# Second feed-forward block: seven half-size block products in place of eight, gated factors through DRAM

## Chip, cores and metric

The kernel runs on one core of a Trainium2 chip. The metric is device time in microseconds (us) from the first to the last instruction of one execution, including what the launch puts around it; of several runs the median is given. A profile of one execution shows TensorE (PE, and PEld for its weight loads), VectorE (DVE), ScalarE (ACT), GpSimd (POOL), and SyncE (SP), which issues nearly all DMAs here.

## What is computed

One encoder block on 1024 tokens of 1024 channels, f32: a feed-forward half, two token mixers (sparse attention and retention), their merge and out projection, a second feed-forward half, a gated embedding, and a final norm. What the change touches, cut from the reference:

```
def swiglu(x, w_gate, w_up, w_down):
    return (jax.nn.silu(x @ w_gate) * (x @ w_up)) @ w_down

h = h + merged @ w_out[i]
h = h + 0.5 * swiglu(rms_norm(h, ffn2_norm[i]), ffn2_w_gate[i], ffn2_w_up[i], ffn2_w_down[i])
gate = jax.nn.sigmoid(rms_norm(h, ple_norm[i]) @ w_ple_gate[i])
h = h + gate * (p[i] @ w_ple_proj[i])
return rms_norm(h, final_norm)
```

`w_gate` and `w_up` are 1024 x 2816, `w_down` 2816 x 1024.

## The kernel before

Every f32 product is made of three matmuls in the format float32r: each operand is split into a high part `h` (a rounded copy, by ACT) and a low part `l` (the rest, by DVE's subtraction), and `split3` (L246) names the three products high x high, high x low, low x high. A matmul takes a stationary 128x128 operand and a moving one of 128x512 and adds into one PSUM bank.

Weights come through the class `Weights` (L86): a list of jobs in the order of use, two raw buffers `wraw` of 128x1024 f32 into which SP loads (L104), and six pairs `wh`, `wl` into which ACT (L117) and DVE (L119, POOL for some jobs) split. When the last product that needs a pair has been issued, `release` gives it back and `pump` loads and splits what is next. PE's instructions stand in the order of the code; the order on the other engines and on SP's queue is set by a scheduler that orders instructions when the program is built.

The activations lie transposed (channels on partitions) in `uh` and `ul`: eight channel blocks by 1024 tokens. `turned` (L322) makes them: four transposes by PE into a bank of the tag `tr` (L328), then the split by ACT and DVE (L250, L251). `Norm.scaled` (L309) is the norm of one block of 128 tokens: ACT squares, a DVE operation, POOL's power, a DVE scaling (L315).

After the merge stage the out projection runs (L1154): for two halves of the channels and eight token blocks, 24 matmuls each (`product`, L288), added into the residual `hres` in SBUF (L1158), which was loaded from `hspill` in DRAM (L1150). In the second half each finished block is normed, and turned two blocks later.

The second FFN is `ffn` (L333), the same code as the first. For each of 22 blocks of 128 hidden units (`gate_up`, L338) and each half of the tokens it makes 24 matmuls for gate (`pg`), 24 for up (`pu`), then Silu on ACT (L354), the product on DVE (L355) and the split into `hh`, `hl`, which stay in SBUF. After every second block `down` (L360) multiplies two blocks into all 8 x 2 pieces of the output, six matmuls each (`pd`), and DVE adds every piece times 0.5 into the residual (L370). The last `down` norms each finished token block and weaves in transposes and the first products of the embedding gate (L1180 to L1185). Then come the embedding gate's products (`ple_gate`, L1170), `embedded`, and `finish` with the final norm and the store.

PSUM's eight banks are dealt out by `bank_plan`: three `mm`, three `dn`, two `tr` in this part.

## Time and profile before

| | |
|---|---|
| three runs | 2720.04, 2723.23, 2723.80 us; median 2723.23 |
| the profiled execution | 2723.87 us, its span 2722.1 us |
| granted TensorE clock, mean | 0.99 of full |
| PE busy | 2645.2 us, 12160 matmuls |
| PEld, DVE, ACT, POOL busy | 2149.6, 1375.9, 872.7, 335.2 us |
| DMA | 190.38 MB, mean 70 GB/s |

The page gives busy time as the union of an engine's instructions. Matmuls overlap in the pipeline and their ends are modelled, so a matmul's duration is longer than the distance to the next one. The chain of the page follows the work that ended last back from the end, from each instruction to what released it. In the views by stretch of time, windows are in us from the start of the span.

### The profile page before, as it was taken

What the parts mean: (1) busy time and instruction counts of PE and PEld (TensorE: products, weight loads), DVE (VectorE), ACT (ScalarE), POOL (GpSimd) and SP (SyncE); (2) the same over time, 40 slices, a digit from 0 to 9 for tenths busy, and PEclk for the clock granted to TensorE, in tenths of its full rate; (3) what the DMA queues carried; (4) which work ended last, traced back from release to release, by engine and by line L of the source; (5) the groups of instructions that cost most, each with busy time, mean ns of one, the idle gap of its engine ahead of it and who ended that gap; (6) DMA issues with size and microseconds to landing.
All of it is one profiled execution on the core that took longest, in us unless ns stands there. A gap on an engine that the chain in (4) does not pass through costs nothing.

```text
span 2722.1 us, 31668 instructions
## 1 busy us (share of the span) xinstructions
PE 2645.2 (97%) x12160; PEld 2149.6 (79%) x12160; DVE 1375.9 (51%) x2622; ACT 872.7 (32%) x1590; POOL 335.2 (12%) x308
## 2 busy tenths in 40 slices
PE   8999999999999998989999999999999999999998
PEld 6888888888888777767878877788888888888877
DVE  5433333333357879997457766524333333333364
ACT  5211111111135667652245654313111111111142
POOL 1000000000000333443344430000000000000000
PEclk9999999999999999999999999999999999999999
DMA  6111111111120221221221228531111111111122
GB/s 237 47 47 47 47 47 47 47 47 47 48 104 20 74 86 32 67 78 55 74 80 39 82 86 236 169 124 55 47 47 47 47 47 47 47 47 47 47 70 93
DMA packets 222487, 190.38 MB, mean 70 GB/s; under 512 B 12416, under 2 KB 186752, under 8 KB 222336
## 3 DMA queue, kind: packets, MB, share of 16 engines
q1 hardware_dynamic: 222336, 188.37, 22.9%
q8 instruction: 95, 1.56, 0.2%
q14 instruction: 56, 0.46, 0.1%
HBM read 154.78 MB, written 33.55 MB: 69 GB/s over the span
## 4 chain that ended last, share of the span: by engine, by line
PE 53%; DVE 8%; issue 3%; ACT 3%; POOL 2%; DMA 1%; SPq 0%; POOLq 0%; ACTq 0%; DVEq 0%
PE prod L288 11%; PE pu L244 9%; PE pg L244 9%; PE pd L244 9%; PE pgate L689 6%; PE pmrg L244 3%; DVE bias L755 1%; PE psc L244 1%; PE plg L244 1%; ACT bias L756 1%; PE ppt L1008 1%; PE ppv L1019 1%; DVE eq L758 1%; DMA sgl<-gspill 1%; DMA yparts<-yaspill 1%
## 5 line engine op out<-in xcount | busy, mean ns | idle before, releaser
L117 ACT ACTIVATE wh<-wraw 128x1024 fp32r<-128x1024 f32 (+1 forms) x224 | 234.4, 1056 | 857.5 <-PE pd L244 405.5
L370 DVE SCALAR_TENSOR_TENSOR hres<-pd,hres 128x512 f32<-128x512 f32 x352 | 240.7, 690 | 200.1 <-PE pd L244 199.5
L119 DVE TENSOR_TENSOR wl<-wraw,wh 128x1024 fp32r<-128x1024 f32 (+1 forms) x176 | 213.8, 1226 | 210.1 <-ACT wh L117 205.6
L355 DVE TENSOR_TENSOR sg<-sg,pu 128x512 f32<-128x512 f32 x88 | 60.5, 687 | 506.6 <-PE pu L244 506.6
L244 PE MATMUL pd<-wh,hh 128*128 128x512 f32 x704 | 279.1, 396 | 0.0
L244 PE MATMUL pg<-uh,wh 128*128 128x512 f32 x704 | 278.6, 396 | 0.2 <-ACT uh L250 0.2
L244 PE MATMUL pg<-ul,wh 128*128 128x512 f32 x704 | 278.5, 396 | 0.2 <-DVE ul L251 0.2
L244 PE MATMUL pu<-uh,wh 128*128 128x512 f32 x704 | 278.5, 396 | 0.0
L244 PE MATMUL pg<-uh,wl 128*128 128x512 f32 x704 | 278.5, 396 | 0.0
L244 PE MATMUL pu<-uh,wl 128*128 128x512 f32 x704 | 278.4, 396 | 0.0
L244 PE MATMUL pu<-ul,wh 128*128 128x512 f32 x704 | 278.4, 395 | 0.0
L244 PE MATMUL pd<-wl,hh 128*128 128x512 f32 x704 | 278.0, 395 | 0.0
L244 PE MATMUL pd<-wh,hl 128*128 128x512 f32 x704 | 278.0, 395 | 0.0
L288 PE MATMUL prod<-wh,uh 128*128 128x512 f32 (+1 forms) x648 | 265.2, 409 | 0.2 <-ACT gt L696 0.2
L288 PE MATMUL prod<-wh,ul 128*128 128x512 f32 (+1 forms) x648 | 257.1, 397 | 0.0
L288 PE MATMUL prod<-wl,uh 128*128 128x512 f32 (+1 forms) x648 | 256.7, 396 | 0.0
L314 POOL TENSOR_TENSOR nst<-nst,mhalf 128x1 f32<-128x1 f32 x32 | 17.9, 559 | 1590.0 <-DVE nst L313 1590.0
L689 PE MATMUL pgate<-uh,wh 128*128 128x512 f32 x384 | 158.7, 413 | 22.2 <-ACT gt L696 21.2
L244 PEld LDWEIGHTS pg<-ul,wh 128*128 128x128 f32 x704 | 132.2, 188 | 32.4 <-DVE ul L251 0.5
L244 PEld LDWEIGHTS pg<-uh,wh 128*128 128x128 f32 x704 | 132.3, 188 | 32.3 <-ACT uh L250 0.5
L244 PEld LDWEIGHTS pu<-uh,wl 128*128 128x128 f32 x704 | 132.2, 188 | 32.0
L244 PEld LDWEIGHTS pu<-ul,wh 128*128 128x128 f32 x704 | 132.2, 188 | 32.0
(225 smaller groups left out, 4684.4 us busy)
## 6 DMA issues: line engine op xcount, KB each, us to landing
wraw<-in_ffn_w_gate_dram SPq DMA_DIRECT2D x44, 512.0 KB, 3.9
wraw<-in_ffn_w_up_dram SPq DMA_DIRECT2D x44, 512.0 KB, 4.7
wraw<-in_ffn_w_down_dram SPq DMA_DIRECT2D x44, 512.0 KB, 3.4
wraw<-in_w_in_dram SPq DMA_DIRECT2D x32, 512.0 KB, 3.8
gspill<-gt SPq DMA_DIRECT2D x48, 256.0 KB, 2.1
wraw<-in_w_branch_b_dram SPq DMA_DIRECT2D x16, 512.0 KB, 4.4
sgl<-gspill SPq DMA_DIRECT2D x32, 256.0 KB, 3.4
wraw<-in_w_in_dram SPq DMA_DIRECT2D x18, 256.0 KB, 3.0
```

The source lines that it names most:

```text
L117: self.nc.scalar.activation(h[:, :n], t[:, :n], AF.Copy)
L119: eng.tensor_tensor(l[:, :n], t[:, :n], h[:, :n].bitcast(F32), op=OP.subtract)
L244: nc.tensor.matmul(ps, a, b, start=i == 0, stop=i == n - 1)
L288: nc.tensor.matmul(box[0][:, :cols], a, w, start=k == 0 and i == 0, stop=k == nk - 1 and i == 2)
L355: nc.vector.tensor_tensor(a, a, pu, op=OP.mult)
L370: nc.vector.scalar_tensor_tensor(hres[:, b, half(i)], pd, 0.5, hres[:, b, half(i)], op0=OP.mult, op1=OP.add)
L689: nc.tensor.matmul(box[0], a, m, start=k == 0 and j == 0, stop=k == KT - 1 and j == 2)
L755: nc.vector.tensor_scalar(m, x_, t[:, j:j + 1], None, op0=op)
L756: nc.scalar.activation(m, m, AF.Copy, accum_out=cnt[:, j:j + 1])
L758: nc.vector.scalar_tensor_tensor(junk[:, : x_.shape[-1]], x_, t[:, j:j + 1], one.to_broadcast([P, x_.shape[-1]]), op0=op, op1=OP.mult, acc ...
L1008: nc.tensor.transpose(ps[:, (t - t0) * P:(t - t0 + 1) * P], L[:, t * P:(t + 1) * P], ident)
L1019: nc.tensor.matmul(pv[:, j].rearrange("p a c -> p (a c)"), vhl[:, s], pT[:, t].rearrange("p a c -> p (a c)"), start=s == 0, stop=s == b)
```

## The change

The second FFN is rewritten with seven products of half-size blocks in place of eight, in a variant that shares its sums (`LEFT` names the seven terms A11, A12, S2, S1, S3, S4, A22). All three matrices are done so: gate and up with a 2x2 cut of the weights (channels by two blocks of 128 hidden units) and of the activations (channels by tokens), down with a 2x2 cut of the gated hidden values and of `w_down`. Gate and up run over 11 pairs of hidden blocks, each matrix in seven terms of 12 matmuls (`term`); the sums of weight blocks are made by POOL in raw buffers (`matrix`), those of activations by POOL after the norm (`turn_second`), turned and kept in `th`, `tl`. The results of one matrix are finished from two running sums `pa` and `pc`: ACT copies a sum out between two terms (`kept`) and DVE adds (`plus`).

The gated values of a pair of hidden blocks are combined by POOL into the seven left factors of down, and these are written to DRAM (`hsp`); the right factors of down, differences of blocks of `w_down`, are made by POOL too and written to DRAM (`wsp`, `down_factors`). Down then runs seven times over all eleven pairs, each time with four sums in four PSUM banks: one step loads a raw buffer with half a left factor and half a right one, splits it like a weight, and makes 12 matmuls (`run`). After each of the seven passes DVE adds the four sums into one or two quarters of the residual (`to`).

Around it: the out projection writes the residual to DRAM (`h2spill`) and norms from blocks that are loaded again, in the order 0, 4, 1, 5, 2, 6, 3, 7; the residual is loaded whole when down begins. Four raw buffers and four weight pairs serve gate and up, seven pairs down. The transposes and the norm of the first four token blocks for the embedding gate stand inside the last pass, those of the other four between the gate's products. Code up to the out projection is as before, apart from where some tiles lie.

The core of the diff:

```diff
+    def matrix(self, key, top, bottom):
...
+        r1 = self.new_load(3, dma(top))
+        r2 = self.new_load(4, dma(bottom))
+
+        def sums(t):
+            gp.tensor_tensor(half(t, 1), part(r1, 1), part(r2, 1), op=OP.add)
+            gp.tensor_tensor(half(t, 0), half(t, 1), part(r1, 0), op=OP.subtract)
+            self.used(r1)
+            self.used(r2)
+
+        t1 = self.new_load(2, sums)
+
+        def differences(t):
+            gp.tensor_tensor(half(t, 0), part(r1, 0), part(r1, 1), op=OP.subtract)
+            gp.tensor_tensor(half(t, 1), part(r2, 0), half(self.raw(t1), 0), op=OP.subtract)
+            self.used(r1)
+            self.used(r2)
+            self.used(t1)
+
+        t2 = self.new_load(1, differences)
...
+        self.fills.append(([r1, r2], False, 2, first))
+        self.fills.append(([t1], False, 2, both(t1, ("S2", "S1"))))
+        self.fills.append(([t2], False, 2, both(t2, ("S3", "S4"))))
+        self.fills.append(([r2], True, 1, last))
...
+    def seven_jobs(name, wg, wu, wd):
+        hsp[name] = [dram.tile([P, 7, 512], F32, name=f"h{name}{j}") for j in range(NJ2)]
+        wsp[name] = [dram.tile([P, 4, 512], F32, name=f"w{name}{j}") for j in range(NJ2)]
+        for j in range(NJ2):
+            for m, w in (("g", wg), ("u", wu)):
+                W.matrix((name, m, j), *(krows(w, 2 * P * j, 2 * P * (j + 1), 4 * q, 4 * q + 4) for q in range(2)))
+        for a in LEFT:
+            for j in range(NJ2):
+                q = LEFT.index(a)
+                t = {"S1": 0, "S2": 1, "S3": 2, "A22": 3}.get(a)
+                if t is None:
+                    f, c = {"A11": (0, 0), "A12": (1, 0), "S4": (1, 512)}[a]
+                    wap = krows(wd, c, c + 512, 2 * j + f, 2 * j + f + 1)
+                else:
+                    wap = wsp[name][j][:, t:t + 1]
+                W.plain((name, a, j), 1, D, False, [(0, 512, hsp[name][j][:, q:q + 1]), (512, D, wap)])
+
     def group_jobs(name, w, cols, nk=KT, step=None, side=False):
...
+        def turn_second(self, i):
+
+            gp = nc.gpsimd
+            f, e = self.x.pop(i), self.x.pop(i + 4)
+            d1, d2, d4 = self.temp("d1"), self.temp("d2"), self.temp("d4")
+            gp.tensor_tensor(d1, e[:, 0:512], f[:, 0:512], op=OP.subtract)
+            gp.tensor_tensor(d2, e[:, 512:D], d1, op=OP.subtract)
+            d3 = e[:, 0:512]
+            gp.tensor_tensor(d3, e[:, 512:D], d3, op=OP.subtract)
+            gp.tensor_tensor(d4, f[:, 512:D], d2, op=OP.subtract)
+            c = tok(i)
+            for n, d in ((1, d2), (0, d1), (2, d3)):
+                self.turned(d, self.th[:, n, :, c], self.tl[:, n, :, c])
+            c = tok(i + 4)
+            self.turned(e[:, 512:D], uh[:, 4:8, c], ul[:, 4:8, c])
+            self.turned(d4, uh[:, 0:4, c], ul[:, 0:4, c])
...
+            def term(ps, key, start, stop):
+                (wh, wl), (bh, bl) = W[key], right[key[1]]
+                for k in range(4):
+                    for i, (x_, y_) in enumerate(split3(wh[:, k], wl[:, k], bh[:, k], bl[:, k])):
+                        nc.tensor.matmul(ps, x_, y_, start=start and k == 0 and i == 0,
+                                         stop=stop and k == 3 and i == 2, skip_group_check=True)
+                W.release(key)
...
+                ps, pc = bank("mm", "pa"), bank("dn", "pc")
+                term(ps, key("A11"), True, False)
+                t = kept(ps)
+                term(pc, key("A12"), True, True)
+                plus(0, t, pc)
+                if m == "g" and j == 0:
+                    between()
+                term(ps, key("S2"), False, False)
+                t2 = kept(ps)
+                pc = bank("dn", "pc")
+                term(pc, key("S1"), True, False)
+                t3 = kept(pc)
+                term(ps, key("S3"), False, False)
+                plus(3, t3, ps)
+                term(pc, key("S4"), False, True)
+                plus(1, t2, pc)
+                term(ps, key("A22"), False, True)
+                use(2, ps)
...
+            for j in range(NJ2):
+                h = g[j % 2]
+                blocks("g", j, silu(h))
+                if j == 0:
+                    self.top.close()
+                    sp = self.top.enter_context(tc.tile_pool(name="hid2", bufs=1, side="right"))
+                    g[1] = [sp.tile([P, 512], F32, name=f"g{i}") for i in range(4)]
+                self.down_factors(sp, j)
+                blocks("u", j, times(h))
+                s1, s2, s4 = (sp.tile([P, 512], F32, name=f"s{i}", tag="s", bufs=4) for i in range(3))
+                gp = nc.gpsimd
+                h11, h12, h21, h22 = h
+                gp.tensor_tensor(s1, h12, h22, op=OP.add)
+                gp.tensor_tensor(s2, s1, h11, op=OP.subtract)
+                gp.tensor_tensor(h12, h11, h12, op=OP.subtract)
+                gp.tensor_tensor(s4, h21, s2, op=OP.subtract)
+                made = dict(A11=h11, A12=h21, S2=s2, S1=s1, S3=h12, S4=s4, A22=h22)
+                for q, n in enumerate(LEFT):
+                    nc.sync.dma_start(hsp[self.name][j][:, q], made[n])
...
+        def down_factors(self, pool, j):
+
+            gp = nc.gpsimd
+            t = pool.tile([P, 2, 2, 512], F32, name="wd", tag="wd", bufs=1)
+            nc.sync.dma_start(t.rearrange("p f i c -> p f (i c)"), krows(self.wd, 0, D, 2 * j, 2 * j + 2))
+            b11, b12, b21, b22 = t[:, 0, 0], t[:, 0, 1], t[:, 1, 0], t[:, 1, 1]
+            gp.tensor_tensor(b11, b12, b11, op=OP.subtract)
+            gp.tensor_tensor(b12, b22, b12, op=OP.subtract)
+            gp.tensor_tensor(b22, b22, b11, op=OP.subtract)
+            gp.tensor_tensor(b21, b21, b22, op=OP.subtract)
+            for q, d in enumerate((b11, b22, b12, b21)):
+                nc.sync.dma_start(wsp[self.name][j][:, q], d)
...
+        def down(self, hres, finished, turn):
+            bank_plan(mm=4, dn=4)
+            sums = [bank("mm", "pda") for _ in range(4)]
+
+            def run(a, ps, start, stop, between=None):
+                for j in range(NJ2):
+                    key = self.name, a, j
+                    h, l = (x[:, 0] for x in W[key])
+                    for i in range(4):
+                        for n, (x_, y_) in enumerate(split3(h[:, tok(i)], l[:, tok(i)], h[:, 512:D], l[:, 512:D])):
+                            nc.tensor.matmul(ps[i], x_, y_, start=start and j == 0 and n == 0,
+                                             stop=stop and j == NJ2 - 1 and n == 2, skip_group_check=True)
+                    W.release(key)
+                    if between and between.get(j):
+                        between[j]()
+
+            def to(ps, t, i):
+                for n in range(4):
+                    r = hres[:, 4 * t + n, half(i)]
+                    nc.vector.scalar_tensor_tensor(r, ps[n], 0.5, r, op0=OP.mult, op1=OP.add)
+
+            run("A11", sums, True, False)
+            to(sums, 0, 0)
+            pc = [bank("dn", "pdc") for _ in range(4)]
+            run("A12", pc, True, True)
+            to(pc, 0, 0)
+            run("S2", sums, False, False)
+            to(sums, 0, 1)
+            pc = [bank("dn", "pdc") for _ in range(4)]
+            run("S1", pc, True, False)
+            to(pc, 1, 1)
+            run("S3", sums, False, False)
+            to(sums, 1, 1)
+            run("S4", pc, False, True)
+            to(pc, 0, 1)
+            bank_plan(mm=4, dn=2, tr=2)
+            finished(0)
+            finished(1)
+
+            def turn_and_next(b):
+                def go():
+                    turn(b)()
+                    if b < 2:
+                        finished(b + 2)
+                return go
+
+            run("A22", sums, False, True, {2 + 2 * b: turn_and_next(b) for b in range(4)})
+            to(sums, 1, 0)
+            finished(4)
+            finished(5)
+
 
...
+    bank_plan(mm=4, dn=2, tr=2)
+    seven = Seven("f2", ffn2_w_down[0], ffn2_norm[0])
+    h2spill = dram.tile([P, NB, D], F32, name="h2spill")
+    W.add(ctx.enter_context(tc.tile_pool(name="raws", bufs=1, side="right")), raws=2)
+    seven.open()
+    W.retire(more)
...
+    for b in range(NB):
+        if b + 2 < NB:
+            ahead[b + 2] = residual(b + 2)
+        ps = product(("o", 0), b, KT)
+        r = ahead.pop(b)
+        nc.vector.tensor_tensor(r, r, ps, op=OP.add)
+        nc.sync.dma_start(h2spill[:, b, 0:512], r)
...
+    order = [b + 4 * e for b in range(4) for e in range(2)]
+    ahead = {b: sums(b) for b in order[:4]}
+    for n, b in enumerate(order):
+        ps = product(("o", 1), b, KT)
+        t = ahead.pop(b)
+        nc.vector.tensor_tensor(t[:, 512:D], t[:, 512:D], ps, op=OP.add)
+        nc.sync.dma_start(h2spill[:, b, 512:D], t[:, 512:D])
+        seven.normed(b)
+        if n >= 2 and n % 2 == 0:
+            seven.turn_first(n // 2 - 1)
+        elif n >= 3:
+            seven.turn_second(n // 2 - 1)
+            for c in order[n + 1:n + 3]:
+                ahead[c] = sums(c)
+    seven.turn_first(3)
+    morex.close()
+
+
+    seven.products(lambda: seven.turn_second(3))
     late = ExitStack()
+    W.add(late.enter_context(tc.tile_pool(name="wlate", bufs=1)), pairs=W_LATE)
+    W.pump()
     rpool = late.enter_context(tc.tile_pool(name="res", bufs=1))
...
-
-
-    finished = normed(ffn2_norm[0], hres)
     for i in range(2):
         for b in range(NB):
-            ps = product(("o", i), b, KT)
-            r = hres[:, b, half(i)]
-            nc.vector.tensor_tensor(r, r, ps, op=OP.add)
-            if i == 1:
-                finished(b)
-                if b >= 2:
-                    turn(b - 2)()
...
+    for b in range(NB):
+        for f in ple_gate(b, 0, tag="mm" if b else "dn"):
+            f()
+        embedded(b, 0, 512, gl.pop(b), 0)
+        if b < 4:
+            turn(b + 4)()
+        if b < 2:
+            finished(b + 6)
```

How instructions now stand on three engines, at the places of which the prediction speaks. In the names, `wh` and `wl` are a pair's high and low part, `wraw` a raw buffer, `ntr` a bank for transposes.

PE, from the last product of the out projection into the first gate product, before:

```order
L288 MATMUL prod<-wh_73,uh 128x512
L288 MATMUL prod<-wl_74,uh 128x512
L288 MATMUL prod<-wh_73,ul 128x512
L328 MATMUL ntr<-ident,xn 128x128 x8
L244 MATMUL pg<-uh,wh_71 128x512
L244 MATMUL pg<-ul,wh_71 128x512
```

and now:

```order
L431 MATMUL prod<-wh_73,uh 128x512
L431 MATMUL prod<-wl_74,uh 128x512
L431 MATMUL prod<-wh_73,ul 128x512
L568 MATMUL ntr<-ident,d_14760 128x128 x4
L568 MATMUL ntr<-ident,d_14759 128x128 x4
L568 MATMUL ntr<-ident,xt 128x128 x8
L568 MATMUL ntr<-ident,d_14761 128x128 x4
L568 MATMUL ntr<-ident,xt 128x128 x8
L608 MATMUL pa<-uh,wh_71 128x512
L608 MATMUL pa<-ul,wh_71 128x512
```

Where eight transposes of one token block stood, there are now 28: five groups of four for the differences of two blocks, and eight for a whole block (`xt` is the normed block, `d` a difference).

POOL, before, from the merge stage to the end, with nothing but powers of the norms in the whole FFN:

```order
L1093 TENSOR_TENSOR yparts<-yparts 128x512 x8
L119 TENSOR_TENSOR wl_72<-wraw_65,wh_71 128x1024
L119 TENSOR_TENSOR wl_76<-wraw_66,wh_75 128x1024
L314 TENSOR_TENSOR nst<-nst,mhalf 128x1 x16
L1212 TENSOR_TENSOR fst<-fst,mhalf 128x1 x8
```

and now, in the second pair of hidden blocks:

```order
L176 TENSOR_TENSOR wraw_65<-wraw_14075 128x512
L680 TENSOR_TENSOR wd<-wd 128x512
L681 TENSOR_TENSOR wd<-wd 128x512
L682 TENSOR_TENSOR wd<-wd 128x512
L663 TENSOR_TENSOR s_15371<-g_14986,g_14988 128x512
L683 TENSOR_TENSOR wd<-wd 128x512
L664 TENSOR_TENSOR s_15372<-s_15371,g_14985 128x512
L168 TENSOR_TENSOR wraw_14076<-wraw_14075,wraw_66 128x512
L665 TENSOR_TENSOR g_14986<-g_14985,g_14986 128x512
L169 TENSOR_TENSOR wraw_14076<-wraw_14076,wraw_14075 128x512
L666 TENSOR_TENSOR s_15373<-g_14987,s_15372 128x512
L177 TENSOR_TENSOR wraw_65<-wraw_66,wraw_14076 128x512
```

POOL now makes sums for the next weights (L168 to L177), factors of `w_down` (L680 to L683) and factors of the gated values (L663 to L666), in one queue and interleaved.

DVE, before, around the additions of one `down`:

```order
L119 TENSOR_TENSOR wl_74<-wraw_66,wh_73 128x1024
L251 TENSOR_TENSOR hl_15997<-sg,hh_15996 128x512
L370 SCALAR_TENSOR_TENSOR hres_14033<-pd,hres_14033 128x512 x16
L119 TENSOR_TENSOR wl_72<-wraw_65,wh_71 128x1024
L119 TENSOR_TENSOR wl_76<-wraw_66,wh_75 128x1024
L355 TENSOR_TENSOR sg<-sg,pu 128x512
```

and now, where the first of down's seven passes ends:

```order
L130 TENSOR_TENSOR wl_17698<-wraw_14075,wh_17697 128x1024
L130 TENSOR_TENSOR wl_17700<-wraw_65,wh_17699 128x1024
L130 TENSOR_TENSOR wl_17702<-wraw_66,wh_17701 128x1024
L130 TENSOR_TENSOR wl_68<-wraw_14075,wh_67 128x1024
L130 TENSOR_TENSOR wl_70<-wraw_65,wh_69 128x1024
L130 TENSOR_TENSOR wl_74<-wraw_66,wh_73 128x1024
L706 SCALAR_TENSOR_TENSOR hres_17718<-pda,hres_17718 128x512 x4
L130 TENSOR_TENSOR wl_17698<-wraw_14076,wh_17697 128x1024
L130 TENSOR_TENSOR wl_17700<-wraw_14075,wh_17699 128x1024
```

The sixteen additions that stood between the splits of a weight and of the next are four now, and the four of the first sum (`pda`) stand ahead of the split of the twelfth step (`wl_17698`), the first one of the second pass.

## Rows read from the trace of the kernel before

**Rows 1.** The page: the span, and busy time, share and instructions of each engine.
```profile
span 2722.1 us, 31668 instructions
...
PE 2645.2 (97%) x12160; PEld 2149.6 (79%) x12160; DVE 1375.9 (51%) x2622; ACT 872.7 (32%) x1590; POOL 335.2 (12%) x308
```

**Rows 2.** Windows, second FFN: length, busy of engines (instructions), granted clock, DMA share, GB/s.
```profile
1871.80:2604.00 732.20, 731.72 (x3149) 588.94 (x3148) 259.91 (x336) 128.39 (x169) 1.65 (x3) 1.00 0.17 50
```

**Rows 3.** The chain around the FFN's start: start us, length us, what.
```profile
1870.95 0.87 PE ntr L328 x8
1871.82 5.60 PE pg L244 x24
...
1883.89 0.45 PE ntr L328 x4
...
1884.36 0.61 ACT uh L250
...
1884.99 0.70 DVE ul L251
...
1936.17 5.60 PE pu L244 x24
```

**Rows 4.** Timeline of PE at the out projection's start: start us, length us, instruction.
```profile
1769.81 0.39 PE L244 MATMUL pmrg<-yh,wl 128*128 128x512 f32 x1
...
1776.61 0.40 PE L244 MATMUL pmrg<-yh,wl 128*128 128x512 f32 x1
1776.84 0.39 PE L288 MATMUL prod<-wh,uh 128*128 128x512 f32 x1
```

**Rows 5.** The chain over the last 120 us: start us, length us, what.
```profile
2608.22 1.16 ACT xn L312 x2
...
2609.70 0.56 POOL nst L314
...
2610.28 1.29 DVE xn L315
...
2646.29 62.32 PE prod L288 x267
```

**Rows 6.** Groups by line, ACT, 1722 to 2722: busy us, mean ns | idle before.
```profile
L117 ACT ACTIVATE wh<-wraw 128x1024 fp32r<-128x1024 f32 x86 | 90.0, 1058 | 442.3 <-PE pd L244 202.7 <-PE pu L244 85.1 <-PE pg L244 82.7
...
L354 ACT ACTIVATE sg<-pg 128x512 f32<-128x512 f32 x44 | 25.9, 590 | 90.0 <-PE pg L244 90.0
```

**Rows 7.** Groups by line, DVE, 1722 to 2722.
```profile
L119 DVE TENSOR_TENSOR wl<-wraw,wh 128x1024 fp32r<-128x1024 f32 x84 | 101.7, 1222 | 102.6 <-ACT wh L117 100.4
L251 DVE TENSOR_TENSOR hl<-sg,hh 128x512 fp32r<-128x512 f32 x44 | 30.3, 688 | 14.7 <-ACT hh L250 14.7
L355 DVE TENSOR_TENSOR sg<-sg,pu 128x512 f32<-128x512 f32 x44 | 30.2, 687 | 258.6 <-PE pu L244 258.6
```

**Rows 8.** Groups by line, POOL, whole span.
```profile
L119 POOL TENSOR_TENSOR wl<-wraw,wh 128x1024 fp32r<-128x1024 f32 x48 | 119.7, 2495 | 207.2 <-ACT wh L117 206.8
...
L698 POOL TENSOR_TENSOR gt<-gt,gnt 128x512 f32<-128x512 f32 x16 | 18.8, 1180 | 73.2 <-ACT gt L696 73.2
...
L1093 POOL TENSOR_TENSOR yparts<-yparts 128x512 f32<-128x512 f32 x8 | 10.6, 1331 | 96.8 <-DMA yparts<-yaspill 96.8
```

**Rows 9.** Timeline of DVE in the branch stage: start us, length us.
```profile
1649.73 1.96 DVE L119 TENSOR_TENSOR wl<-wraw,wh 128x1024 fp32r<-128x1024 f32 x1 [0.26 <-ACT wh L117]
```

**Rows 10.** Timeline of POOL at the same time.
```profile
1649.29 1.32 POOL L1093 TENSOR_TENSOR yparts<-yparts 128x512 f32<-128x512 f32 x1 [1.20 <-DMA yparts<-yaspill]
```

**Rows 11.** Windows while the residual is loaded.
```profile
1784.00:1788.00 4.00, 4.00 (x19) 3.22 (x18) 0.69 (x1) 0.00 (x0) 0.00 (x0) 1.00 1.01 393
1788.00:1792.00 4.00, 4.00 (x18) 3.19 (x17) 0.69 (x1) 0.00 (x0) 0.00 (x0) 1.00 1.03 417
```

**Rows 12.** DMA issues: count, KB each, median us to landing.
```profile
sgl<-gspill SPq DMA_DIRECT2D x32, 256.0 KB, 3.4
```

**Rows 13.** Timeline of SP's queue in the branch stage: start us, length us.
```profile
1731.24 0.41 SPq L1122 DMA_DIRECT2D sgl<-gspill  x1
```

More of the change, by code (lines that the diff above doesn't have):

```diff
@@ L99, in load @@
     def load(self):
-        key, k, c, side, pieces = self.jobs[self.loaded]
         t = self.raw_free.pop(0)
-        v = t[:, : k * c].rearrange("p (k c) -> p k c", k=k)
-        for c0, c1, ap in pieces:
-            self.nc.sync.dma_start(v[:, :, c0:c1], ap)
-        self.raw.append((key, k, c, side, t))
+        self.loads[self.loaded][2] = t
         self.loaded += 1
+        self.loads[self.loaded - 1][1](t)
     def pump(self):
@@ L111, in pump @@
                 self.load()
[L112 removed]
+            if self.filled == len(self.fills):
                 return
[L114 to L121 removed]
+            needs, half, n, fill = self.fills[self.filled]
+            if max(needs) >= self.loaded or not (self.free or half and self.half_open):
+                return
+            if half and self.half_open:
+                slot, part, self.half_open = self.half_open, 1, None
+            else:
+                slot, part = self.free.pop(0), 0
+                if half:
+                    self.half_open = slot
+            slot.live += n
+            self.filled += 1
+            for key, views in fill(slot, part):
+                self.pair[key] = slot, views
     def __getitem__(self, key):
@@ L126, in release @@
     def release(self, key):
-        self.free.append(self.pair.pop(key)[0])
+        slot = self.pair.pop(key)[0]
+        slot.live -= 1
+        if slot.live == 0:
+            if self.half_open is slot:
+                self.half_open = None
+            if slot.kept:
+                self.free.append(slot)
         self.pump()
```

215 lines of the change are left out of this document (165 added, 50 removed).

## Prediction

> **What bounds the kernel now.** I read the page first: TensorE is busy 97% of the span at the full granted level [rows 1]. That busy time counts pipelined matmuls whose ends are modelled, so I then checked by starts. In the windows view the stretch of the second FFN holds 731.72 us of PE in 732.20, at granted clock 1.00, that is 2.4 GHz [rows 2]. The chain says what one matmul costs there: 24 of `pg`, and as many of `pu`, take 5.60 us [rows 3], so 0.2333 us from start to start (the 396 ns that the page gives as mean of one are latency, and no sum may use them). Four transposes take 0.45 us, eight 0.87 [rows 3].
>
> With these two prices the last part of the program can be counted. From the first `prod` of the out projection (1776.84 [rows 4]) to the end of the last `prod` of the embedding gate (2646.29 + 62.32 = 2708.61 [rows 5]) lie 931.8 us. The code issues 384 matmuls for the out projection, 3168 for the FFN (22 column blocks x 2 halves x 8 x 3 for gate, the same for up; 11 x 16 x 6 for down) and 384 for the gate: 3936 x 0.2333 = 918.4 us, and 32 groups of four transposes x 0.44 = 14.1. The sum, 932.5, leaves nothing for waiting. So every matmul removed here is worth its 0.2333 us, until something else ends last. The 13.5 us from 2708.6 to the end are the last block's evacuation and store, and stay.
>
> **What is removed.** Each 2x2 block product takes seven half products in place of eight: gate and up have 22 pairs x 7 terms x 12 = 1848 matmuls for 2112, down 7 x 11 x 12 = 924 for 1056. That is 2772 for 3168: 396 x 0.2333 = **-92.4 us**. Down also loses 148 of its 176 DVE accumulations into the residual (28 are left, since a sum stays in PSUM over all eleven pairs). They were hidden behind PE, so I put them at nothing.
>
> **What is added on PE.** Transposes rise from 64 to 112 ahead of the FFN (the differences of token blocks are transposed too): 12 groups x 0.44 = **+5.2 us**. Matmuls and transposes together: 932.5 becomes 845.3.
>
> **New waits in the turning.** `turn_second` sends five groups of four through two `tr` banks. A bank comes back after the transposes 0.45, the ACT copy 0.61, the DVE subtraction 0.70 [rows 3] and some 0.1 of handing over: 1.85 us. So groups three to five wait, and between them ACT also squares a block (1.16) and DVE scales one (1.29) [rows 5]. Walking the two queues through, I get 4.6 us for the five groups in place of 2.2: 2.4 us, three times inside the projection, 7.2. The third has `turn_first` right behind (order excerpt: 28 transposes in a row): +1.8, and the first gate term needs their last pieces, +1.4, a wait like the one already there at 1884 [rows 3]. The fourth, inside the first gate product, meets the weight splits and the first Silu: +4. Sum **+14 us**. Bounds: 0, as the eights of today pass without a wait [rows 3]; and 37, if each of 28 groups waited for a whole evacuation, 28 x 1.31.
>
> **Gate and up.** A term is 12 matmuls, 2.8 us; a matrix is 19.6, a pair of matrices 39.2. Evacuations hide: a bank is written again one term later, and in that 2.8 us lie an ACT split (1.058) and a copy (0.590) [rows 6], and on DVE a split (1.222) and an addition (0.687) [rows 7]. Three of the four weight slots come free inside the running matrix, and their contents are made a matrix ahead, so a late load has some 10 us. The new worker is POOL: per pair 4 operations for each matrix and 4 for the gated factors, 128x512 each, which the trace has at 1180 and 1331 ns [rows 8]; at 1.25 that is 20 us of 39.2. But the order excerpt shows that the 44 operations on the down weights are crowded into the first pairs; the second to fourth pair hold 23 or 24 operations, 30 us. And POOL and DVE hold each other up: the split at 1649.73 took 1.96 us for its usual 1.222 [rows 7, 9], and ended 1.1 us, about one split, after a POOL addition that had begun just before it [rows 10]. DVE operations with both inputs in SBUF make 4 x 1.222 + 6 x 0.69 + 3 x 0.69 = 11.1 us a pair. Serial with 30 us that is 41, 2 us over the pair, three times, against 10 us of lead: I take **+3 us**. Bounds: 0, when the lead covers it; 29, at the 1.57 us that one addition would need to cost (24 x 1.57 + 11.1 = 48.8, 9.6 over, three times, no lead).
>
> The Trainium skill says the same as a rule (SBUF — State Buffer, section Who interferes with whom): a DVE instruction with two SBUF inputs contends with a GpSimd instruction that reads SBUF, and the second one blocks until the first is done. The trace agrees, with the 1.96 us. By that rule alone, taken as a full serialisation without any lead, the time is the 2681 us of the first rival below; by the row with the lead it is the 2655 of my sum.
>
> **Down.** Each of 77 steps takes one 512 KB pair (half factor, half weight) and 12 matmuls, 2.8 us, so 187 GB/s. The residual was loaded at 417 GB/s with the queues full [rows 11], so the rate is there. A raw buffer's round is two issues of 0.41 us [rows 13], a landing of 3.4 [rows 12], split 1.058 and 1.222: 6.5 us for four buffers, or 1.6 a step, below 2.8. One wait I do expect: the order excerpt puts DVE's four additions of the first sum ahead of the split of the twelfth step, so PE waits the last addition and that split, 0.7 + 1.2 = **+2 us**, once. Bounds 0 and 11: the residual's 4 MB pass the same queue first, 10.7 us at 393 GB/s [rows 11]; where SP is late by all of it, so is the step. What goes through DRAM I put at nothing: in a pair SP moves 2 MB of weights, 1.8 MB of factors and at first 2 MB for the down weights, 5.9 MB in 39.2 us or 150 GB/s, beside PE's terms; a factor written in the last pair is read in the eleventh step, 28 us later, against a landing of 3.4. SP issues 312 more DMAs, 128 us at 0.41, spread over some 850 us; without that cover a late factor would cost its landing once, 3 to 4 us. The residual's detour through `h2spill` lies beside products of 5.6 us in the same way. After `A22` the normalisation of block 4 (1.16 + 0.56 + 1.29 [rows 5]) hides behind a gate product of 5.6 us.
>
> **Sum.** -92.4 + 5.2 + 14 + 3 + 2 = -68.2; the count stood 0.7 above the measured 931.8, which I neglect. Span 2722.1 - 68.2 = 2653.9; the profiled execution took 2723.87, 1.8 more, so 2655.7; it stands 0.6 above the median of the three runs, 2723.23. So **2655 us**.
>
> **Rivals.**
> *POOL and DVE, one at a time, starve the first pairs.* For it: the stretched split [rows 9, 10] and 23 to 24 operations in three pairs. Against: the lead, and that only 16 operations stand in the later pairs. By the upper bound, 29 in place of 3: 2681 us.
> *The port makes it slower than before.* The same lock in all eleven pairs: if a POOL addition of 512 columns cost, with its waits, what the split of 1024 columns costs today, 2495 ns [rows 8], a pair would need 16 x 2.5 + 11.1 = 51 us, 12 over, eleven times: 2655 - 3 + 131 = 2783 us. It turns at 2.15 us an operation: 16 x 2.15 + 11.1 = 45.5, 6.4 over, which eats the 71 us. Against: no row of 512 columns has a mean over 1331.
> *The new operands stream faster.* `pmrg` matmuls of the same shape start every 6.80/30 = 0.2267 us [rows 4]; what makes the difference the trace doesn't say, and the new halves lie elsewhere in SBUF. 2772 x 0.0067 = 18 us less: 2637.
> *Down waits for its loads.* If each pair landed after 10.7 us, a whole residual's load at the rates of [rows 11], the round is 13.8 us, 3.45 a step, 0.65 over, 77 times, 50 us: 2705.
>
> **Numbers.** Forecast 0.72; the first rival 0.13; faster streaming 0.06; loads 0.04; the slower one 0.05. The range reaches from 2636 (the faster streaming) to 2690 (the first rival, with some of the turning's upper bound). About 0.2%, 5 us, is what a measurement here can tell from no change. All cases but one lie far below that, and of the slower one I give a hundredth to its turning point: faster 0.95, same 0.01, slower 0.04.
>
> **What would show it.** In the profile after: `pa` and `pc` terms of 2.8 us without idle time of PE between matrices, 431 us for the 22 of them; some 5 us for each `turn_second`; 31 us for each of the seven sums of down, 216 together, and 2 us of idle PE after the first; in all about 20 us of idle PE between the first `prod` of the projection and the last. It is wrong if POOL additions of the factors average over 1.6 us and `ev` or `wh` waits stand ahead of PE in the waits view, if ACT's split waits for DMA in down, or if matmuls start at another spacing than 0.233.

## The result, and the profile after

The changed kernel takes 2691.6 us (2689.99 to 2692.14) against 2722.8 for the kernel before in the same session: ratio 0.9886, interval 0.9869 to 0.9903. It is faster, by 31 us where 68 were forecast, and 1.6 us outside the range. The profiled execution has a span of 2690.0 us. Its page, against [rows 1]:

```profile
span 2690.0 us, 32204 instructions
...
PE 2567.0 (95%) x11812; PEld 2088.5 (78%) x11812; DVE 1454.1 (54%) x2631; ACT 987.4 (37%) x1745; POOL 615.2 (23%) x498
```

PE's share fell from 97% to 95%: of its 78 us of busy time less, 32 came off the span. POOL nearly doubled.

The windows view of the profile after, cut at the bounds of the stages (length, then busy time and count of PE, PEld, DVE, ACT and POOL, granted clock, DMA share, GB/s): out projection with turning; gate and up to the end of the waits; the rest of gate and up; down.

```profile
1782.86:1897.64 114.78, 104.08 (x477) 83.63 (x477) 50.06 (x65) 27.85 (x47) 34.15 (x30) 0.96 0.34 110
1897.64:2110.00 212.36, 183.61 (x742) 145.22 (x742) 94.67 (x90) 59.92 (x92) 140.21 (x95) 0.92 0.53 183
2110.00:2371.11 261.11, 261.11 (x1129) 211.85 (x1128) 115.12 (x133) 89.97 (x133) 108.76 (x73) 1.00 0.34 108
2371.11:2588.49 217.38, 214.25 (x957) 176.59 (x956) 123.48 (x123) 93.82 (x98) 8.03 (x8) 1.00 0.68 221
```

The stages against the forecast, each from its first matmul to the next one's (products at 0.2333 us, groups of four transposes at 0.44, plus the waits that the prediction allowed):

| stage | forecast | measured | off |
|---|---|---|---|
| first `prod` of the out projection, after the start | 1776.84 | 1782.86 | +6.0 |
| out projection and turning (384 products, 23 groups, 10.4 of waits) | 110.1 | 114.8 | +4.7 |
| gate and up (1848 products, 5 groups, 7 of waits) | 440.4 | 473.5 | +33.1 |
| down (924 products, 8 groups, 2 of waits) | 221.1 | 217.4 | -3.7 |
| embedding gate | 93.1 | 93.0 | -0.1 |

That is 40.0 us. The span lies only 36 above the forecast 2653.9, for the prediction's count had a slip: the chain [rows 5] leaves PE at 2708.61, but PE starts its last matmul at 2713.96. The count of 932.5 stands against 937.1, not 931.8, and so is 4.6 us short: PE already stood 3.5 us there in the kernel before, and the sum, made by differences, carried the shortfall along.

Nearly everything is gate and up. In its first 212 us PE stands 28.8, at a mean clock of 0.92; the 261 us behind them have no idle time. The waits view of that first stretch, for PE and then for POOL and ACT (engine, line, waited for: us, times, longest):

```profile
PE pa L608 <- ACT ev L619: 22.8, 6, 7.7
PE pc L608 <- ACT ev L619: 3.1, 2, 2.5
```
```profile
POOL wd L680 <- DMA wd<-in_ffn_w_down_dram: 49.1, 11, 8.0
```
```profile
ACT wh L128 <- DMA wraw<-in_ffn_w_up_dram: 36.6, 4, 13.5
ACT wh L128 <- DMA wraw<-in_ffn_w_gate_dram: 24.4, 4, 7.9
...
ACT wh L128 <- POOL wraw L169: 15.2, 4, 5.8
```

PE waits for `ev`, the copy of a full bank, and ACT waits for raw weights. The timelines of SP's queue, ACT and PE around one of these gaps (start, length, instruction, in brackets the idle time before it):

```profile
2013.60 0.43 SPq L685 DMA_DIRECT2D wf<-wd  x1
2014.13 0.40 SPq L156 DMA_DIRECT2D wraw<-in_ffn_w_gate_dram  x1
2014.58 0.56 SPq L685 DMA_DIRECT2D wf<-wd  x1
2019.47 0.38 SPq L678 DMA_DIRECT2D wd<-in_ffn_w_down_dram  x1
2019.96 0.40 SPq L156 DMA_DIRECT2D wraw<-in_ffn_w_gate_dram  x1
```
```profile
2017.50 0.61 ACT L646 ACTIVATE g<-ev 128x512 f32<-128x512 f32 x1
2025.95 0.63 ACT L128 ACTIVATE wh<-wraw 128x512 fp32r<-128x512 f32 x1 [7.84 <-DMA wraw<-in_ffn_w_gate_dram]
2026.49 0.58 ACT L646 ACTIVATE g<-pa 128x512 f32<-128x512 f32 x1
2026.97 0.62 ACT L128 ACTIVATE wh<-wraw 128x512 fp32r<-128x512 f32 x1
2027.49 0.59 ACT L619 ACTIVATE ev<-pa 128x512 f32<-128x512 f32 x1
```
```profile
2024.65 0.39 PE L608 MATMUL pc<-uh,wl 128*128 128x512 f32 x1
2028.13 0.50 PE L608 MATMUL pa<-th,wh 128*128 128x512 f32 x1 [3.09 <-ACT ev L619]
```

Read from the end: PE starts at 2028.13 because the bank's copy `ev` (2027.49) was late. The copy stood in ACT's queue behind splits of the next gate weight (2025.95), for whose second half ACT had waited 7.84 us. That half had been issued on SP only at 2019.96, right behind a `wd` load (2019.47), which SP held until the last factor's store (`wf<-wd`, 2014.58) had landed. The weight was for the next matrix; the copy was needed at once.

### The profile page after: what moved, and what is told of

Its sections match the earlier page's. It is cut to its first block, busy times and chain, and to the rows that moved or that the text cites. A ratio compares the mean times of both kernels' runs of the same rounds, so it can differ in the third digit from the quotient of the medians.

```text
span 2690.0 us, 32204 instructions
## 1 busy us (share of the span) xinstructions
PE 2567.0 (95%) x11812; PEld 2088.5 (78%) x11812; DVE 1454.1 (54%) x2631; ACT 987.4 (37%) x1745; POOL 615.2 (23%) x498
## 4 chain that ended last, share of the span: by engine, by line
PE 43%; DVE 8%; POOL 6%; DMA 5%; issue 5%; ACT 3%; SPq 0%; POOLq 0%; ACTq 0%; DVEq 0%
PE prod L431 12%; PE pgate L1046 6%; PE pa L608 5%; PE pmrg L387 4%; PE pc L608 3%; PE pda L697 3%; PE pdc L697 3%; DMA wd<-in_ffn_w_down_dram 2%; DVE bias L1112 1%; DMA wf<-wd 1%; ACT bias L1113 1%; PE psc L387 1%; PE ppt L1365 1%; PE ppv L1376 1%; PE plg L387 1%
## 5 line engine op out<-in xcount | busy, mean ns | idle before, releaser
L130 DVE TENSOR_TENSOR wl<-wraw,wh 128x1024 fp32r<-128x1024 f32 (+1 forms) x299 | 364.1, 1224 | 380.5 <-ACT wh L128 377.2
L1046 PE MATMUL pgate<-ul,wh 128*128 128x512 f32 x384 | 153.2, 399 | 0.0
L1046 PE MATMUL pgate<-uh,wl 128*128 128x512 f32 x384 | 152.8, 398 | 0.0
L387 PE MATMUL pd<-wh,hh 128*128 128x512 f32 x352 | 139.6, 397 | 0.0
L387 PE MATMUL pg<-uh,wh 128*128 128x512 f32 x352 | 139.3, 396 | 0.0
L387 PE MATMUL pu<-uh,wl 128*128 128x512 f32 x352 | 139.2, 396 | 0.0
L387 PE MATMUL pu<-uh,wh 128*128 128x512 f32 x352 | 139.2, 396 | 0.0
L387 PE MATMUL pu<-ul,wh 128*128 128x512 f32 x352 | 139.2, 396 | 0.0
L387 PE MATMUL pg<-ul,wh 128*128 128x512 f32 x352 | 139.2, 395 | 0.0
L387 PE MATMUL pg<-uh,wl 128*128 128x512 f32 x352 | 139.2, 395 | 0.0
```

What stands on the lines that cost most here:

```text
L130: eng.tensor_tensor(l, src, h.bitcast(F32), op=OP.subtract)
L387: nc.tensor.matmul(ps, a, b, start=i == 0, stop=i == n - 1)
L1046: nc.tensor.matmul(box[0], a, m, start=k == 0 and j == 0, stop=k == KT - 1 and j == 2)
```

## The experiments

e1, e7, e8 and e10 ran four times, and their median is given; the others ran once, so that a few us between two of them tell little. What a stage took is read from the profiled execution.

**e1, e2, e4, e5: what in the crowd costs.** Three readings were open: POOL's queue stands for the single `wd` buffer; POOL and DVE hold each other up (the first rival); the extra bytes are in the way.

e1:
```diff
+                with (tc.issue_after(done) if j else ExitStack()):
-                self.down_factors(sp, j)
+                    self.down_factors(sp, j)
...
-                gp.tensor_tensor(s4, h21, s2, op=OP.subtract)
+                done = gp.tensor_tensor(s4, h21, s2, op=OP.subtract).ins
```
(`issue_after` queues what its block puts on the same engine behind the given instruction.)

> The four factor operations of each hidden pair are queued on POOL behind the last gated-factor operation of the pair before, so that POOL holds 16 operations of 512 columns in every pair, where the change has 23 or 24 in the second to fourth pair and 12 from the sixth on. Theory 'POOL's queue waits' (in the change POOL stands 49 us for the 11 loads of the one wd buffer, and the sums of the next weights queue behind it): the waits go, gate and up take 433 us in place of 467.6, the half-clock stretches behind the gaps go too, 2658 us in all. Rival 'POOL and DVE hold each other up whenever both work': the same work on both engines, spread, so gate and up stay over 455 us, 2680 us or more. Rival 'the extra transfers themselves are in the way': the same bytes, also 2680 or more.

2680.85 us, ratio 0.9834 (0.9818 to 0.9851). Gate and up fell only from 473.5 to 468.8; the rest of the gain is an earlier start of the out projection (1777.6). So crowding and POOL's wait for `wd` are not the main thing. The loss is now 2 to 5 us in nearly every pair.

e2:
```diff
-            gp.tensor_tensor(b11, b12, b11, op=OP.subtract)
-            gp.tensor_tensor(b12, b22, b12, op=OP.subtract)
-            gp.tensor_tensor(b22, b22, b11, op=OP.subtract)
-            gp.tensor_tensor(b21, b21, b22, op=OP.subtract)
```

> The four POOL operations on each down weight are left out (the raw blocks go through DRAM in their place, so the down sums are others); loads and stores of wd stay, crowded early. Theory 'POOL's queue waits': nothing on POOL waits for wd any more, gate and up 433 us, 2658 us in all, equal to e1. Rival 'the extra transfers are in the way': over 2680, as the transfers are all there and come faster one after the other. Rival 'POOL and DVE lock': 2658 too, so this run tells only the transfers apart.

2658.44 us, gate and up 440.1. The bytes are not in the way; the four operations, or what waits for them, are. That e1 did not come out equal, as the first theory wanted, already speaks against that theory.

e4:
```diff
-            t = pool.tile([P, 2, 2, 512], F32, name="wd", tag="wd", bufs=1)
+            t = pool.tile([P, 2, 2, 512], F32, name="wd", tag="wd", bufs=2)
...
-                s1, s2, s4 = (sp.tile([P, 512], F32, name=f"s{i}", tag="s", bufs=4) for i in range(3))
+                s1, s2, s4 = (sp.tile([P, 512], F32, name=f"s{i}", tag="s", bufs=3) for i in range(3))
```

> A second wd buffer (and three s buffers for four, which makes the room), so that a load of wd runs while POOL works on the other one. The scheduler now sets eight factor operations in a row at several places and is done within four pairs. Theory 'POOL's queue waits for loads': the 49 us of waiting on POOL fall below 15, and PE's idle time in the first five pairs from 29 to some 10 us, about 2668 us. Rival 'too many POOL operations in few pairs, locked with DVE': as many operations in fewer pairs, so the idle time stays or grows, 2690 or more.

2684.19 us. POOL's wait for `wd` loads fell from 49.1 to 21.9 us, and gate and up only to 464.8: a miss for the first theory.

e5, on top of e1:
```diff
+            for _ in range(8):
+                gp.tensor_tensor(pool.tile([P, 512], F32, name="scr", tag="scr", bufs=1), b11, b12, op=OP.add)
```

> e1 and eight more POOL additions of 512 columns in each pair, into a scratch tile that nothing reads: 24 operations in each of the 11 pairs, as in the crowded pairs of the change, but without a wait for a load in their midst. Theory 'POOL's queue waits for loads': 24 x 1.27 to 1.6 us = 30 to 38 us of a pair of 39, so little is lost, 2658 to 2670 us. Rival 'too many POOL operations, locked with DVE': 8 to 10 us more in each of 11 pairs, 2750 us or more.

2790.28 us, as the rival had it. But the trace shows another reason: the additions read `wd`, and so the next `wd` load, and with it SP, waits for the last of them. SP's queue of e5, where nothing is issued for 11 us:

```profile
2121.41 2.83 SPq L688 DMA_DIRECT2D wf<-wd  x3
2135.29 0.38 SPq L679 DMA_DIRECT2D wd<-in_ffn_w_down_dram  x1
2135.76 0.42 SPq L156 DMA_DIRECT2D wraw<-in_ffn_w_gate_dram  x1
```

e5 therefore told the two apart as little as e1 did. What e1 and e5 share is a gate load behind a `wd` load. New theory: **SP's queue stands.** In these traces it issues in order; a store that waits for POOL, or a `wd` load that waits for a store to land, holds back weight loads behind it, and ACT, in order as well, holds a bank's copy behind the split of such a weight.

**e6, e7: the same POOL work, another order on SP.** e6 is e1 with the two buffers of e4.

> e1 with a second wd buffer (and three s buffers for four). POOL's order and its 16 operations a pair are those of e1; what goes is SP's wait: in e1 the load of the next wd stands in SP's queue until the stores of the last one have landed (2129.93, against the last store at 2127.5), and the load of a gate weight stands behind it. Theory 'SP's queue stands': a good part of the 28.6 us of gaps of e1 goes (some 2.4 us in each of 10 pairs), 2660 us; what may stay is the wait for the three wf stores ahead of the gate load. Rival 'POOL and DVE hold each other up': the same operations, 2680 us as e1.

2674.91 us, gate and up 465.8: 3 us for the 24 expected. In its SP queue three stores (1994.08 to 1995.76) and the `wd` load (1997.66) still stand ahead of the second gate load (1998.14): it is the place in the queue that would have to change, not the buffer. Inconclusive by itself.

e7 moves places in the queue (with e4's buffers and e1's `done`), and makes the factors of each pair one pair later:
```diff
-                self.down_factors(sp, j)
+                if j:
+                    self.down_factors(sp, j - 1, done)
...
+            with tc.issue_after(done):
                 gp.tensor_tensor(b11, b12, b11, op=OP.subtract)
...
+            with tc.issue_after(W.sent):
                 for q, d in enumerate((b11, b22, b12, b21)):
                     nc.sync.dma_start(wsp[self.name][j][:, q], d)
```
`W.sent` is the last gate or up load put on SP; the last pair's factors follow behind the loop.

> e6 with another order of SP's queue: the four wf stores and the next wd load are queued behind both loads of the next gate weight, in place of between and ahead of them. POOL and DVE do the same work, 16 POOL operations in each pair. Theory 'SP's queue stands': no weight load waits for POOL any more, a pair takes 38.9 us as the late pairs of the change do, gate and up 436 to 441 us in place of 473.5, the whole 2655 us. Rival 'POOL and DVE hold each other up': 16 operations in all pairs cost what they cost in e1, 2675 to 2681 us.

2653.98 us, ratio 0.9743 (0.9728 to 0.9757). SP's queue of e7 in one pair, and the windows view over gate and up of the change, of e1 and of e7:

```profile
2105.40 4.99 SPq L157 DMA_DIRECT2D wraw<-in_ffn_w_gate_dram  x2
2110.48 2.57 SPq L691 DMA_DIRECT2D wf<-wd  x4
2116.94 0.38 SPq L682 DMA_DIRECT2D wd<-in_ffn_w_down_dram  x1
2120.24 0.38 SPq L157 DMA_DIRECT2D wraw<-in_ffn_w_up_dram  x1
```
```profile
1897.64:2371.11 473.47, 444.72 (x1869) 357.07 (x1869) 209.79 (x223) 149.88 (x225) 248.97 (x168) 0.97 0.42 142
```
```profile
1892.50:2361.30 468.80, 442.99 (x1870) 355.81 (x1870) 207.18 (x223) 149.33 (x225) 251.56 (x168) 0.98 0.43 143
```
```profile
1893.30:2329.50 436.20, 433.40 (x1870) 351.12 (x1870) 194.31 (x223) 151.37 (x225) 242.59 (x164) 0.99 0.45 151
```

POOL does the work of e1 (251.6 and 242.6 us, the last pair's factors falling into down), PE's idle time goes from 25.8 us (e1) to 2.8, and PE's busy time from 443.0 to 433.4: with the gaps went most of the stretches at the lower level. Both gate loads stand ahead of the stores, and no weight waits for POOL; among ACT's waits in gate and up no DMA is left. 433.4 is what the prediction had for matmuls and transposes in this stage (431.2 + 2.2).

Outside gate and up, e7 begins the out projection 3.0 us earlier (1779.8) and turns in 113.5 us for 114.8, but its down takes 222.3 us for 217.4. The stores of the last pair's factors now stand ahead of loads that down needs, and PE stands 5.2 us there, once:

```profile
2336.70 5.45 SPq L691 DMA_DIRECT2D wf<-wd  x4
2342.24 0.38 SPq L139 DMA_DIRECT2D wraw<-hf  x1
```

**e11: the rival by itself.** e7 with one `wd` buffer and eight more POOL additions a pair on a tile of their own, four behind `done`, four behind the last sum for the next weight:
```diff
+            for at in (done, W.summed):
+                with tc.issue_after(at):
+                    for _ in range(4):
+                        gp.tensor_tensor(scr, scr, scr, op=OP.add)
```

> e7 (one wd buffer) and eight more POOL additions of 512 columns in every pair, on a scratch tile that no transfer and no other engine touches: 24 in each of 11 pairs as in the crowded pairs of the change, and with the SP order of e7, so that no load waits for them. What e5 should have told and could not, since its additions read wd and so held the next load back. Theory 'SP's queue stands, the number of POOL operations is harmless': 24 x 1.3 to 1.5 = 31 to 36 us fit into 38.9, pairs of 38.9 to 40 us, 2655 to 2668 us. Rival of the prediction 'POOL and DVE one at a time': 36 + 11 = 47 us a pair, 8 over, ten times: 2735 us.

2657.04 us, every pair from the second on 38.9 us as in e7. The windows view over gate and up of e11, and groups by line (busy us, mean ns | idle before), of POOL in e11 and in e7, and of DVE in e11 and in e7:

```profile
1892.10:2327.70 435.60, 432.79 (x1869) 350.61 (x1869) 215.23 (x224) 151.30 (x224) 355.22 (x244) 0.99 0.46 152
```
```profile
L178 POOL TENSOR_TENSOR wraw<-wraw 128x512 f32<-128x512 f32 x18 | 32.3, 1795 | 0.0
```
```profile
L178 POOL TENSOR_TENSOR wraw<-wraw 128x512 f32<-128x512 f32 x19 | 24.9, 1308 | 45.9 <-DMA wraw<-in_ffn_w_up_dram 45.9
```
```profile
L651 DVE TENSOR_TENSOR g<-g,ev 128x512 f32<-128x512 f32 x32 | 35.6, 1112 | 0.8
```
```profile
L651 DVE TENSOR_TENSOR g<-g,ev 128x512 f32<-128x512 f32 x32 | 22.1, 689 | 0.8
```

POOL is busy 355 of 436 us and PE stands for 2.8. POOL and DVE do stretch each other: one of the four operations for a weight (L178) takes 1.80 us where e7 has 1.31, the product with `ev` 1.11 for 0.69. At 24 operations a pair that is hidden in gate and up. Down is 4.2 us longer than in e7 (226.4 for 222.3); the chain there runs through the extra additions of the last pair.

**e8, e9, e12, e10: the turning, the merge, the start of down.** e8 is e7 with
```diff
-    bank_plan(mm=4, dn=2, tr=2)
+    bank_plan(mm=3, dn=2, tr=3)
...
-        seven.normed(b)
         if n >= 2 and n % 2 == 0:
             seven.turn_first(n // 2 - 1)
         elif n >= 3:
             seven.turn_second(n // 2 - 1)
+        seven.normed(b)
+        if n >= 3 and n % 2:
```

> e7 with three banks for transposes and three for products (two and four in the change), and with the transposes of a finished block put ahead of the squares of the next one in the out projection. Theory 'turn_second waits for its banks, and for an ACT square between its copies': each turn_second in the out projection takes 3.5 us in place of 5, the long one ahead of the first gate product 8 in place of 11; out projection and turning 109 us in place of 114.8, so 5 to 6 us below e7. Rival 'the turning waits for POOL' (the power of the last norm stands behind sums of weights there): only the short ones gain, 2 to 3 us. Rival 'the clock': the half-clock stretches of 3 to 7 us that follow the gaps stay, and with them over half of the loss: under 2 us.

2646.5 us, ratio 0.9715 (0.9698 to 0.9731). The windows view of e8 over out projection and turning, and over gate and up:

```profile
1776.70:1881.80 105.10, 101.12 (x476) 81.51 (x475) 48.38 (x65) 28.10 (x48) 30.08 (x26) 1.00 0.36 120
1881.80:2322.90 441.10, 434.53 (x1871) 351.94 (x1869) 196.27 (x226) 152.21 (x225) 247.72 (x168) 0.99 0.45 150
```

105.1 us for 114.8, idle 4.0 for 10.7, clock 1.00 for 0.96. But a part of the wait only moved behind the cut: the first gate product now waits 3.4 us, and gate and up take 441.1 us where e7 has 436.2. Both stages together take 546.2 us for e7's 549.7, 3.5 less. Another 3.1 come from an earlier start of the out projection (1776.7 for 1779.8), which nothing in the edit explains, so that the expected size was met in part by luck. The short turns gained (two waits of 0.54 us, for 1.07 and 0.81 in each of two turns of the change), the long one hardly, as the rival with POOL had it: the power of the last norm (1883.21) stands on POOL behind four operations for weights (1877.07 to 1883.25). Which of the two edits helped the short turns was not tried.

e9 is the kernel before, unchanged.

> The kernel before, unchanged, for a second profile of it. In the change the out projection began 6.0 us later than in the kernel before (1782.86 for 1776.84), in e1 0.8 us later, in e2 3.7, in e4 7.2, with the same instructions on PE, DVE and ACT up to there. Theory 'the merge stage varies from run to run' (landing of yparts and sgl): here too it begins anywhere from 1775 to 1784. Theory 'the change's two early gate loads in SP's queue do it': it begins at 1777 again, within 1 us.

Span 2722.2 us, the out projection at 1776.92, as the second theory had it. e12 is the change with this around the load of a gate or up half:
```diff
+                with (self.tc.issue_after(self.hold) if self.hold else ExitStack()):
```
where `hold` is the last residual load, until the turning ends.

> The change, with one thing altered: the FFN's first two gate loads are queued on SP behind the residual loads of the out projection. In the change they are issued at 1681.4, in the middle of the merge stage, and the out projection begins at 1782.9, 6 us later than in both profiles of the kernel before (1776.84, 1776.92). Theory 'the early loads delay the merge': it begins within 1.5 us of 1777, and the whole takes 2686 us. Rival 'the merge differs from program to program for another reason' (it began anywhere from 1774.6 to 1784.0 in seven kernels with these loads): anywhere in that range, with no relation to the loads.

2689.23 us; the out projection began at 1777.7, as the first theory said. But e6 began at 1774.6 and e1 at 1777.6 with the early loads, and the change came out of the merge's first wait at 1654.03, the kernel before at 1652.34, before those loads were issued (1681.4). The 6 us at the start stay open.

e10 is e8 with the hold of e12 and the factors one pair earlier:
```diff
-                if j:
-                    self.down_factors(sp, j - 1, done)
+                self.down_factors(sp, j, done if j else W.summed)
```

> e8 with two more changes. The down weight of a pair is factored one pair earlier than in e7 and e8 (the first one while the first up product runs), so that nothing on POOL or SP stands ahead of down's first loads; and the first two gate loads of the FFN are queued on SP behind the last residual loads of the out projection, not in the merge stage. Theory 'SP's queue stands' again at the start of down (in e8 the four wf stores of the last pair hold back the loads of the fifth step, PE idle 4.3 us): that gap falls below 2 us, 4 us less. For the early loads in the merge: e8 begins the out projection at 1776.7 already, so 0 to 2 us. Together 2640 to 2643 us. Rival: the wait only moves to another step of down or of the first pair, which now has four factors more on POOL, and the time stays within 2 us of e8's 2646.5.

2642.58 us, ratio 0.9706 (0.969 to 0.9722): the lowest median of the study, 49 us below the change (its interval overlaps e8's). PE's idle time in down fell from 4.4 us (e8) to 2.0, and down from 220.9 us to 216.3, the 4 us expected.

## Why the prediction was wrong

- **Removed work, -92.4 us: right.** In e7 gate and up take 433.4 us of PE for the forecast 433.4, and all later pairs of the change 38.9 us for 39.2. That the first two agree to the digit is partly chance: eleven pairs at 0.3 us less are 3.3 us, and about as much goes at the lower clock level in e7's first pair, which takes 47.2 us.
- **Turning, +14: right in place, and in mechanism for the short turns; short by the clock.** PE stood 10.7 us in out projection and turning, for 10.4 forecast; 5.6 of them are waits for a bank's evacuation. The chain of the changed kernel at the first `turn_second` shows the walk of the prediction, with ACT's squares between the copies:

```profile
1851.18 0.45 PE ntr L568 x4
...
1851.65 0.29 ACT th L393
...
1852.15 1.14 ACT sq L560 x2
1853.29 0.50 ACT th L393
...
1853.81 0.70 DVE tl L394
...
1854.55 1.82 PE ntr L568 x8
```

  The last turn ahead of the first gate term has a wait of 3.1 us that the walk does not hold. The power of the last norm (`nst`) stands on POOL behind sums of weights, and the scaling and the transposes wait for it:

```profile
1890.76 1.60 POOL wraw L169
1892.36 0.52 POOL nst L562
...
1892.90 2.27 DVE xt L563
1895.18 0.61 DVE ul L394
...
1895.84 1.97 PE ntr L568 x8
```

  So the size of 10.4 is in part luck. Of the 4.7 us missed, 4.4 are matmuls at the granted level 1.2 GHz: the stage's mean clock is 0.96, and its PE time 104.1 where matmuls and transposes count 99.7. No term held this. In gate and up it is 11.3 us (444.7 for 433.4). The row of [rows 2], at 1.00, says only that a stage without gaps keeps its level.
- **Gate and up, +3: the step that failed.** The prediction put "what goes through DRAM" at nothing, as bytes beside PE's terms and issues of 0.41 us, and held that "a late factor would cost its landing once". It did count the queue's rate, and not its order. On SP the stores wait for POOL, and ten of the eleven `wd` loads for the stores of the one before, and weight loads stand behind both; on ACT the copies that free a bank stand behind splits of those weights. The "10 us of lead" was lead of the weight, which was real, and not of the copy. PE stands 28.8 us, 25.9 of them for `ev`, and its matmuls take 11.3 us more at the lower level: 40.1 us where the table allows 7, so 33.1 over. e7 gives back 37.3 in this stage, by order and a second `wd` buffer, which e11 shows not to be needed there.
- **The first rival, 2681 us, had the place and nearly the size, and the wrong cause.** It named the crowded pairs; the change lost its time in pairs one to five. Its sign came only by half: PE did wait for `ev`, but POOL's operations for the factors (L663 to L666 and L680 to L683 of the change) average 1.55 us, not over 1.6. And e11 runs 24 operations in every pair from the second to the tenth at no cost in gate and up, so the lock doesn't set the time there. The slower rival falls with it. The rule of the Trainium skill that stands behind both (SBUF — State Buffer, section Who interferes with whom), that a DVE instruction with two SBUF inputs contends with a GpSimd instruction that reads SBUF, agrees with single instructions of e11 (the product with `ev`, 1.11 us for 0.69).
- **Down, +2: right in place and size, its cause not told apart; and its matmuls were dearer in the sum than on the chip.** The A11 to A12 wait was 1.8 us (gaps of 0.71 and 1.59 from start to start at 2403, less two matmuls). The split does stand directly behind the four additions, as forecast (2401.53 to 2404.26, the split at 2404.18). But its load was late too: ACT had waited 8.4 us for it until 2402.74, behind the residual's loads on SP, and by these times the late load alone would have cost some 1.5 us. Another wait of 2.2, not forecast, came at the start of the fifth step. In the chain 132 matmuls of `pda` take 29.92 us, 0.2267 each:

```profile
2435.45 29.92 PE pda L697 x132
```

  924 x 0.0067 = 6 us less than forecast. So the third rival was right for down, and in a smaller measure for the 66 terms of gate and up on `th` (2.75 us for 2.80, 3.3 us in all).
- **Down waits for its loads:** on ACT, hardly on PE. ACT's splits wait 22.6 us for loads of `w_down`, twelve times, which was one of the signs of being wrong; but PE stands 3.1 us in 217, while 221 GB/s are moved.

## What to carry to other kernels

Ask of each DMA that a change adds not only what it moves, but what it waits for, and what stands behind it in its queue: a store that waits for a slow engine belongs behind the loads that someone else needs. Do the same for the engine that empties PSUM banks: a split that may wait for a load should not stand ahead of a copy for which PE waits. (This half is read from the trace; no run moved ACT's order alone.) Where a scheduler sets the order, look in its listing for such neighbours; here a few ordering edges were worth 37 us, more than the change itself had brought (31). And look again after the cure: e7's own stores held up down, and e8's turning waits for one small POOL operation behind four large ones.

## What had not been expected of the hardware

- Gaps of PE cost more than themselves. Of the six over 2 us in gate and up of the change, four (3.1 to 7.7 us) came with 3 to 10 us at the lower level (granted clock 0.50), from within the gap or right behind it, and two (2.4 and 2.5 us) with none. That is 11.3 us in gate and up on top of 28.8 of standing, and 4.4 in the turning on top of 10.7. With the gaps most of it went too (e7, e8).
- Matmuls of one shape stream at three rates: 0.2267 us in down and merge, 2.75 us for 12 (0.2292) with the differences `th`, 2.80 (0.2333) with `uh`. The chain of the changed kernel:

```profile
2251.80 5.60 PE pa L608 x24
2257.39 2.80 PE pc L608 x12
2260.20 2.75 PE pa L608 x12
```

  What of the operands makes the difference was not tried.
- Two profiles of the kernel before begin the out projection within 0.1 us of each other (1776.84 and 1776.92), while eleven programs with the changed kernel's code up to there (three of them with other early loads or another deal of banks) begin it between 1773.2 and 1784.0.
